# One core, a two-layer trunk in split float32: instructions recorded and issued in an order computed in the kernel, in place of the program's own order

## The chip, the cores and the metric

The kernel runs on one core of one Trainium2 chip. The metric is the device time of one execution in microseconds, the median of several runs.

Engine names as in the profile: PE is TensorE's matmul, PEld its weight load, DVE VectorE, ACT ScalarE, POOL GpSimd, SP SyncE, which here only issues DMAs. Each engine has an instruction queue of its own and works through it in order; an instruction that has to wait for another engine holds up what stands behind it on its own engine.

## The reference

Sequence 512, model width 1024, two layers, each a mixer followed by a SwiGLU FFN (hidden width 2816), each in front of a residual addition and behind an RMSNorm, and one RMSNorm at the end. The first mixer is a gated MLP whose gate mixes positions within chunks of 128, the second is retention with four heads. Everything is float32.

```python
for i in range(2):
    hn = rmsnorm(h, mix_norm_g[i])
    h = h + (sgu_mixer(hn, ...) if i == 0 else retention(hn, ...))
    h = h + swiglu(rmsnorm(h, ffn_norm_g[i]), ffn_w_gu[i], ffn_w_down[i])
return rmsnorm(h, final_norm_g)

# sgu_mixer: u, v = split(gelu(hn @ w_in)); v = layernorm(v); (u * (causal w_s @ v + b_s)) @ w_out
# retention: q, k, v, g = split(hn @ w_in); rotary(q), rotary(k); decayed causal attention by head;
#            (norm(o) * gn_g * silu(g)) @ w_out
# swiglu:    a, b = split(hn @ w_gu); (silu(a) * b) @ w_down
```

## The kernel before

**Split operands.** Each float32 operand is split in two: a high half, a copy rounded to the type that PE takes at its full pace (`fp32r`), made by ACT, and a low half, operand minus high half, made by DVE. Names with `wh_`/`wl_` are a weight's halves, `wr_` the raw weight, `XH`/`XL` those of the normed and transposed activations, `z_P6h`/`z_P6l` and the like those of sums of activations. `three` (lines 246 to 249) issues three matmuls for each pair of blocks: high by high (L247), and the two mixed products (L248, L249).

**Seven products.** A large product is done in quarters with seven block products instead of eight (`seven`): P1, P7, P6, Q4, P5, P2, P3. Each adds into one of three PSUM accumulators, X, Y and Z (in the last layer also W), and needs sums of weight blocks (P7 two blocks, P6 three, Q4 four, P5 two) and sums of activation quarters (S1 to S4; `z_S1`, `z_S2` in retention's output product). A weight sum is made either by DVE from two loaded tiles (`plus`, L377), or by an accumulating DMA which POOL issues onto the tile that holds the block before (`add`, L349), after the product that read that tile has made its halves. Plain loads go through SP (`load`, L346). All weight tiles come from one pool of 38 tiles of 4 KB a partition.

**Stages.** The SGU mixer: products `v0`, `v1`, `u0`, `u1` and the mixing, then `so`, which adds into the residual X. FFN 0: six units `gu0_0` to `gu0_5`, then `dn0_0` and `dn0_1`, which add into X. Retention: per head queries and keys (`qk`), values and gate (`vg`), scores, `pv`, then `zT`, the transpose of the gated result, then `ro`, which adds into X. FFN 1: `gu1_*`, `dn1_0`, `dn1_1`; its end norm runs by chunks inside the last product (`apart`), and the result is stored.

**The turn.** In front of each layer the residual of a chunk of 128 rows is scaled (`xs_f0_3` for chunk 3 in front of FFN 0), transposed by PE in eight pieces into PSUM (`xT_f0_3`), and copied out (`turn`, L667 to L672): ACT makes XH's columns, DVE XL's, both from PSUM, and for FFNs and retention `raw_copy` (L704) makes two float32 copies `xr`, from which the sums of activation quarters are built. These copies free the PSUM bank.

**What sets the order.** The program issues work as jobs with leads: `pipeline` calls a weight's load 8 jobs ahead of its product, its high half 6, its low half 5, its sum 7, an accumulating DMA 8 and more. Products follow one of four written orders (`ORDER`, `LATER`, `FIRST`, `SPREAD`). The order of the instructions that results is then scheduled again by the framework (`schedule_with_timeline_sim=True`), which moves instructions within the limits of their dependences, and gives each engine its queue.

Of the kernel before, what the change touches and what calls it, by code (L numbers as in the profile page):

```python
# [32 lines left out]
N_GEN = 38  # L33
N_TMP = 5
# [22 lines left out]
class Job:  # L57
# [34 lines left out]
def pipeline(jobs):  # L92
    weighted = [j for j in jobs if j.steps]
    leads = sorted({n for j in weighted for n, _ in j.steps})
    at = dict.fromkeys(leads, 0)
    done = 0
    for job in jobs:
        for n in leads if done else leads[::-1]:
            while at[n] < min(len(weighted), done + n):
                for m, step in weighted[at[n]].steps:  # L100
                    if m == n:
                        step()
                at[n] += 1
        if job.steps:
            done += 1
        if job.work:
            Chain.all_step()
        job.run()


@with_exitstack
def trunk(ctx, tc, x, positions, mix_g, ffn_g, fin_g, sgu_w_in, sgu_w_s, sgu_b_s, sgu_ln_g, sgu_ln_b,
          sgu_w_out, ret_w_in, ret_gn_g, ret_w_out, ffn_w_gu, ffn_w_down, invf, decay, out):
    nc = tc.nc
    const = ctx.enter_context(tc.tile_pool(name="const", bufs=1))
# [35 lines left out]
    def f32(t):  # L151
        return t.bitcast(F32)
# [6 lines left out]
    late = []  # L159
# [3 lines left out]
            late.pop(0)()  # L163

    ident = const.tile([P, P], F32, name="ident")
    make_identity(nc, ident)
# [84 lines left out]
    xn = {}  # L251
# [265 lines left out]
    def into_x(name, w, groups, A, ready=None, mid=None, look=3, halves=(0, 1), apart=False):  # L517

        norm = chunk_norm(name, ready, with_gain if apart else None) if ready else None
        by_dma = norm and sum(len(up) for up, low in groups) == 4

        def plus(i, j, ps, op, cs=(0, 1)):
            c0 = 2 * halves[i]
            q = X[:, c0 + cs[0]:c0 + cs[-1] + 1, j * T:(j + 1) * T]
            nc.vector.tensor_tensor(q, q, ps[:, cs[0]:cs[-1] + 1, :], op)

        def dma_plus(q, i, j, ps, sign):
            t = G(f"{q}_{name}")  # L530
# [132 lines left out]
    def turn(c, src, name, more=None):  # L663

        ps = PS(f"xT_{name}_{c}", (P, KD, P))
        for k in range(KD):
            xn["turned"] = nc.tensor.transpose(ps[:, k, :], src[:, k * P:(k + 1) * P], ident)  # L667
# [3 lines left out]
        nc.scalar.activation(xn["h"][:, :, cs], ps, AF.Copy)  # L671
# [23 lines left out]
    XR = {}  # L695

    def raw_copy(name):

        def copy(c, ps):
            if (name, c // 2) not in XR:  # L700
                XR[name, c // 2] = [G(f"xr_{name}_{c // 2}_{j}", F32, (P, 4, H)) for j in range(2)]
            cs = slice((c % 2) * P, (c % 2 + 1) * P)
            for j in range(2):
                nc.scalar.activation(XR[name, c // 2][j][:, :, cs], ps[:, 4 * j:4 * j + 4, :], AF.Copy)  # L704
# [124 lines left out]
    v = [[None, None] for _ in range(2)]  # L829
# [149 lines left out]
    def mix(j, half):  # L979
        for i in (2 * half, 2 * half + 1):  # L980
# [10 lines left out]
            if i % 2 == 1:  # L991
# [288 lines left out]
    t = [list(range(4 * hd, 4 * hd + 4)) for hd in range(HEADS)]  # L1280
# [39 lines left out]
```

## Time and profile before

| what | value |
|---|---|
| median of 3 runs | 1202.3 us (1201.9 to 1203.36) |
| the profiled execution's own time | 1203.41 us |
| its span | 1201.7 us, 18455 instructions |
| mean granted clock of PE | 0.996 |
| PE busy | 1180.0 us, 98% |
| DVE, ACT, POOL busy | 960.9 (80%), 664.6 (55%), 171.0 us (14%) |
| bytes moved by DMA | 225.90 MB, 188 GB/s over the span |

The span is the time from the first instruction to the last of one profiled execution; the profiled execution's own time has what lies around that span as well. A busy share is an average over stages that wait for different things. Where PE idles, the profile names the engine, line and tile that ended the wait (the "waits"), and the granted clock (1.00 is full speed) shows whether a busy PE is also a fast one.

### The profile page before, as it was taken

To read this page: it belongs to the slowest core of one execution; us is meant where nothing else is said; L and a number is where in the kernel's file an instruction comes from. 1 tells how busy PE (TensorE), PEld (TensorE's weight loads), DVE (VectorE), ACT (ScalarE), POOL (GpSimd) and SP (SyncE) were. 2 spreads that over 40 slices of the span, in tenths; PEclk is the share of its full clock that TensorE was granted. 3 is DMA by queue.
4 is the path that set the end of the run, shared out by engine and by line. 5 is a ranking of instruction groups with operands and counts; after the bars stand their busy time and mean duration, and the time that the engine had idled before them with its cause. 6 is when DMAs were issued, how large, how long until landed. Compare 5 with 4: busy or idle time off the path is not lost.

```text
span 1201.7 us, 18455 instructions
## 1 busy us (share of the span) xinstructions
PE 1180.0 (98%) x7374; PEld 1067.4 (89%) x7374; DVE 960.9 (80%) x1143; ACT 664.6 (55%) x842; POOL 171.0 (14%) x151
## 2 busy tenths in 40 slices
PE   8999999999999999999999999999999999999997
PEld 7888899989999987988989898878899989999986
DVE  5587998899977789787885959879788896676897
ACT  5523775554444547555664656566565545535465
POOL 1000122121010130110201111220121210101210
PEclk9999999999999999999999999999999999999999
DMA  9912878898684898777677868877868887856892
GB/s 314 282 47 59 244 161 182 226 228 208 160 205 108 225 184 265 176 163 184 155 202 178 192 155 203 183 151 247 217 153 211 186 216 210 199 135 192 168 245 97
DMA packets 128167, 225.90 MB, mean 188 GB/s; under 512 B 7464, under 2 KB 30032, under 8 KB 128080
## 3 DMA queue, kind: packets, MB, share of 16 engines
q1 hardware_dynamic: 88848, 153.37, 38.6%
q0 software_dynamic: 38944, 70.81, 35.3%
q8 instruction: 58, 0.95, 0.3%
q10 hardware_dynamic: 288, 0.52, 0.1%
q14 instruction: 29, 0.24, 0.1%
HBM read 221.53 MB, written 2.10 MB: 186 GB/s over the span
## 4 chain that ended last, share of the span: by engine, by line
PE 85%; DMA 5%; issue 4%; DVE 2%; ACT 2%; POOL 1%; SPq 0%; DVEq 0%; POOLq 0%; ACTq 0%
PE X_gu L247 6%; PE X_gu L249 6%; PE X_gu L248 6%; DMA wr_gu_P<-in_ffn_w_gu 3%; PE Y_gu L249 3%; PE Y_gu L248 3%; PE Y_gu L247 3%; PE X_dn L247 3%; PE X_dn L248 3%; PE X_dn L249 3%; PE X_vg L247 2%; PE X_vg L248 2%; PE X_vg L249 2%; PE ps_v L247 1%; PE Y_dn L248 1%
## 5 line engine op out<-in xcount | busy, mean ns | idle before, releaser
L216 ACT ACTIVATE wh_gu_P<-wr_gu_P 128x1024 fp32r<-128x1024 f32 x132 | 135.3, 1053 | 87.6 <-DVE wr_gu_P L377 51.0
L223 DVE TENSOR_TENSOR wl_gu_P<-wr_gu_P,wh_gu_P 128x1024 fp32r<-128x1024 f32 x132 | 158.7, 1219 | 25.4 <-ACT wh_gu_P L216 25.1
L349 POOL DMA_DIRECT2D wr_gu_P<-in_ffn_w_gu x50 | 60.9, 1258 | 414.0 <-DVE wl_gu_P L223 196.2
L216 ACT ACTIVATE wh_dn_P<-wr_dn_P 128x1024 fp32r<-128x1024 f32 x72 | 69.1, 980 | 42.6 <-DMA wr_dn_P<-in_ffn_w_down 17.8
L223 DVE TENSOR_TENSOR wl_dn_P<-wr_dn_P,wh_dn_P 128x1024 fp32r<-128x1024 f32 x72 | 79.4, 1128 | 2.7 <-issue 1.1
L223 DVE TENSOR_TENSOR wl_vg_P<-wr_vg_P,wh_vg_P 128x1024 fp32r<-128x1024 f32 x48 | 57.8, 1217 | 14.5 <-ACT wh_vg_P L216 14.4
L349 POOL DMA_DIRECT2D wr_dn_P<-in_ffn_w_down x36 | 41.9, 1239 | 143.6 <-DVE wl_dn_P L223 46.6
L216 ACT ACTIVATE wh_vg_P<-wr_vg_P 128x1024 fp32r<-128x1024 f32 x48 | 49.2, 1055 | 22.8 <-DMA wr_vg_P<-in_ret_w_in 16.7
L349 POOL DMA_DIRECT2D wr_vg_P<-in_ret_w_in x26 | 31.5, 1248 | 207.5 <-DMA wr_vg_P<-in_ret_w_in 73.8
L247 PE MATMUL X_gu<-XH_f,wh_gu_P 128*128 128x256 f32 x176 | 50.6, 288 | 2.2 <-ACT xr_f L704 2.2
L247 PE MATMUL Z_gu<-XH_f,wh_gu_P 128*128 128x256 f32 x176 | 50.0, 284 | 1.4 <-DVE s L1051 1.4
L247 PE MATMUL X_gu<-xP5h_f,wh_gu_P 128*128 128x256 f32 x176 | 50.0, 284 | 0.9 <-ACT u L1026 0.9
L249 PE MATMUL Y_gu<-XH_f,wl_gu_Q 128*128 128x256 f32 x176 | 49.9, 284 | 0.8 <-DVE wl_gu_Q L223 0.8
L248 PE MATMUL X_gu<-XL_f,wh_gu_P 128*128 128x256 f32 x176 | 50.5, 287 | 0.0
L249 PE MATMUL X_gu<-XH_f,wl_gu_P 128*128 128x256 f32 x176 | 50.5, 287 | 0.0
L247 PE MATMUL X_gu<-xP6h_f,wh_gu_P 128*128 128x256 f32 x176 | 50.0, 284 | 0.2
L247 PE MATMUL Y_gu<-XH_f,wh_gu_Q 128*128 128x256 f32 x176 | 49.9, 284 | 0.0
L249 PE MATMUL Z_gu<-XH_f,wl_gu_P 128*128 128x256 f32 x176 | 49.9, 283 | 0.0
L248 PE MATMUL X_gu<-xP6l_f,wh_gu_P 128*128 128x256 f32 x176 | 49.8, 283 | 0.0
L249 PE MATMUL X_gu<-xP3h_f,wl_gu_P 128*128 128x256 f32 x176 | 49.8, 283 | 0.0
L248 PE MATMUL X_gu<-xP3l_f,wh_gu_P 128*128 128x256 f32 x176 | 49.8, 283 | 0.0
L249 PE MATMUL X_gu<-xP6h_f,wl_gu_P 128*128 128x256 f32 x176 | 49.8, 283 | 0.0
(643 smaller groups left out, 4284.5 us busy)
## 6 DMA issues: line engine op xcount, KB each, us to landing
wr_gu_P<-in_ffn_w_gu SPq DMA_DIRECT2D x110, 512.0 KB, 5.3
wr_gu_P<-in_ffn_w_gu POOLq DMA_DIRECT2D x50, 512.0 KB, 7.8
wr_dn_P<-in_ffn_w_down SPq DMA_DIRECT2D x50, 512.0 KB, 5.5
wr_vg_P<-in_ret_w_in SPq DMA_DIRECT2D x40, 512.0 KB, 5.8
wr_dn_P<-in_ffn_w_down POOLq DMA_DIRECT2D x30, 512.0 KB, 7.3
wr_vg_P<-in_ret_w_in POOLq DMA_DIRECT2D x26, 512.0 KB, 6.9
wr_ro_P<-in_ret_w_out SPq DMA_DIRECT2D x20, 512.0 KB, 4.8
wr_qk_P<-in_ret_w_in SPq DMA_DIRECT2D x15, 512.0 KB, 5.9
```

Of the source, the lines that this page charges most:

```text
L216: nc.scalar.activation(h, s, AF.Copy)
L223: nc.vector.tensor_tensor(l, s, f32(h), ALU.subtract)
L247: nc.tensor.matmul(o, ah, bh, start=start, stop=False, skip_group_check=True)
L248: nc.tensor.matmul(o, ah, bl, start=False, stop=False, skip_group_check=True)
L249: return nc.tensor.matmul(o, al, bh, start=False, stop=stop, skip_group_check=True)
L349: nc.gpsimd.dma_start(raw[p, 0, g, s][:, 0:nk, :], source(b, g, s, nk), accum_op=ALU.add)
```

## The change

Three edits.

1. **Order.** Every call on an engine is recorded instead of issued (`Recorder`, `EngineProxy`, `record`); tiles are stand-ins (`Virtual`, `View`) which know who reads and writes which part. At the end, `emit` computes an order from fixed costs for each kind of instruction and issues all of it in this order, with the framework's own scheduling off. The order is made in two passes. Backward from PE's program order, every other operation gets the latest time at which it may end (`late`). Then a forward pass plays the engines against each other: PE takes the lowest program number among what is ready; the others the operation with the least `late`; at most 8 DMAs each on SP and on POOL are taken to be under way; a transfer counts as landed 2000 (the pass counts in ns) after its planned landing, so that its readers stand later in their queues. Tiles of a pool are granted in this order too. The waits themselves are still semaphores: the numbers only set the order of the queues. In the changed kernel the recorded operations all bear the line 332.

```diff
+HW_DMAS = 8
+LATE = 2000
...
+        else:
+            q = min(active, key=lambda q: q[0][1])
+            op = q.pop(0)[0]
+            op.end = now
+            post(now + LATE, op)
...
+                if e == "PE":
+                    op = min((o for o in queue[e] if can(o)), key=lambda o: o.n, default=None)
+                else:
+                    for o in queue[e]:
+                        if can(o):
...
+                            cost = o.late + (3 * TABLE if o.table and o.table != table else 0)
+                            if op is None or (cost, o.n) < best:
+                                op, best = o, (cost, o.n)
...
+def emit(rec):
+    with rec.tc.manual_schedule():
+        for op in order_of(rec):
+            op.call()
...
     pipeline(jobs)
+    emit(rec)
```

2. **XL from copies.** Where a turn also makes `xr` copies (the turns f0, r and f1, four chunks each), XL's columns are no longer made from PSUM by one DVE subtraction of 1024 columns but from the two `xr` copies in SBUF by two of 512.

```diff
         nc.scalar.activation(xn["h"][:, :, cs], ps, AF.Copy)
-        nc.vector.tensor_tensor(xn["l"][:, :, cs], ps, f32(xn["h"][:, :, cs]), ALU.subtract)
-        if more is not None:
-            more(c, ps)
+        if more is None:
+            nc.vector.tensor_tensor(xn["l"][:, :, cs], ps, f32(xn["h"][:, :, cs]), ALU.subtract)
+        else:
+            more(c, ps, cs)
...
-                nc.scalar.activation(XR[name, c // 2][j][:, :, cs], ps[:, 4 * j:4 * j + 4, :], AF.Copy)
+                nc.scalar.activation(own[j], ps[:, 4 * j:4 * j + 4, :], AF.Copy)
+            for j in range(2):
+                js = slice(4 * j, 4 * j + 4)
+                nc.vector.tensor_tensor(xn["l"][:, js, cs], own[j], f32(xn["h"][:, js, cs]), ALU.subtract)
```

3. **The last product's P5.** In `dn1_1` the sum of two blocks for P5 is made by an accumulating DMA onto a tile of its own instead of by a DVE addition: four DVE additions fewer, four POOL DMAs more.

```diff
-            made = seven(name, w, groups, 0, T, A, evac, mid, look, order=order, dma=("P7",), onto=("P6", "Q4"), apart=apart,
+            made = seven(name, w, groups, 0, T, A, evac, mid, look, order=order, dma=("P7", "P5") if apart else ("P7",), onto=("P6", "Q4"), apart=apart,
```

Of instructions, the matmuls and SP's loads are the same in number; ACT has 17 table loads instead of 14.

What the order became at three places. DVE at the second half of retention's output product (`ro`): `sg3_*` are the last head's gated results, `X_95` (`X_82` in the changed kernel) is the residual, `z_S1_1`, `z_S2_1` and `z_P6l_1` are what P6's second half needs. Before:

```order
L1236 SCALAR_TENSOR_TENSOR sg3_0_7406<-pv3_0_7607,nf5_o3_0_7626,sg3_0_7406 128x512 x2
L527 TENSOR_TENSOR X_95<-X_95,Y_ro_7684 128x2x512
L223 TENSOR_TENSOR wl_ro_P6_1_0_7700<-wr_ro_P722_1_0_7431,wh_ro_P6_1_0_7699 128x1024
L480 TENSOR_TENSOR z_S1_1_7749<-z2_1_7009,z3_1_7714 128x1024
L480 TENSOR_TENSOR z_S2_1_7751<-z_S1_1_7749,z2_0_7023 128x1024
L223 TENSOR_TENSOR wl_ro_P6_1_2_7745<-wr_ro_P722_1_2_7457,wh_ro_P6_1_2_7744 128x1024
L506 TENSOR_TENSOR z_P6l_1_7748<-z_S2_1_7751,z_P6h_1_7747 128x1024
```

After:

```order
L332 SCALAR_TENSOR_TENSOR sg3_1_7497<-pv3_1_7558,nf5_o3_1_7688,sg3_1_7497 128x512 x2
L332 SCALAR_TENSOR_TENSOR sg3_0_7556<-pv3_0_7581,nf5_o3_0_7690,sg3_0_7556 128x512 x2
L332 TENSOR_TENSOR wl_ro_P6_1_0_7718<-wr_ro_P722_1_0_7433,wh_ro_P6_1_0_7703 128x1024
L332 TENSOR_TENSOR z_S2_0_7637<-z_S2_0_7637,z1_0_6397 128x1024
L332 TENSOR_TENSOR X_82<-X_82,s1_ro_7684 128x2x512
L332 TENSOR_TENSOR z_S1_1_7758<-z2_1_7037,z3_1_7734 128x1024
L332 TENSOR_TENSOR wl_ro_Q4_0_0_7769<-wr_ro_P722_0_0_7330,wh_ro_Q4_0_0_7752 128x1024
L332 TENSOR_TENSOR z_S2_1_7776<-z_S1_1_7758,z2_0_7057 128x1024
L332 TENSOR_TENSOR wl_ro_P6_1_2_7785<-wr_ro_P722_1_2_7512,wh_ro_P6_1_2_7760 128x1024
L332 TENSOR_TENSOR X_82<-X_82,Y_ro_7669 128x2x512
L332 TENSOR_TENSOR z_P6l_1_7803<-z_S2_1_7776,z_P6h_1_7790 128x1024
```

The addition of Y_ro to the residual stood ahead of z_S1 and z_S2 and now stands behind them, directly in front of z_P6l. On PE, Y_ro's second P7 half and the first P6 half of X_ro (24 matmuls each) stand between the transposes of the last head and the product that reads z_P6l_1.

ACT at the turn into FFN 1 (`f1`): the copies out of the transposes of the last two chunks, `xT_f1_0` and `xT_f1_1`. Before:

```order
L671 ACTIVATE XH_f1_8143<-xT_f1_0_8370 128x8x128
L216 ACTIVATE wh_gu1_1_P1_0_2_8302<-wr_gu1_1_P111_0_2_8229 128x1024
L216 ACTIVATE wh_gu1_1_P2_0_0_8333<-wr_gu1_1_P221_0_0_8237 128x1024
L1026 ACTIVATE s1_1_0_8361<-X_gu1_0_8307 128x1024
L216 ACTIVATE wh_gu1_1_P2_0_2_8364<-wr_gu1_1_P221_0_2_8305 128x1024
L704 ACTIVATE xr_f1_0_0_8381<-xT_f1_0_8370 128x4x128
L671 ACTIVATE XH_f1_8143<-xT_f1_1_8446 128x8x128
L704 ACTIVATE xr_f1_0_1_8382<-xT_f1_0_8370 128x4x128
L216 ACTIVATE wh_gu1_0_P7_0_0_8411<-wr_gu1_0_P722_0_0_8231 128x1024
L1052 ACT_TABLE_LOAD
L1052 ACTIVATE s1_1_0_8361<-s1_1_0_8361 128x1024
L216 ACTIVATE wh_gu1_0_P7_0_2_8443<-wr_gu1_0_P722_0_2_8239 128x1024
```

After:

```order
L332 ACTIVATE s1_1_0_8395<-X_gu1_0_8284 128x1024
L332 ACTIVATE XH_f1_8189<-xT_f1_0_8392 128x8x128
L332 ACTIVATE xr_f1_0_0_8416<-xT_f1_0_8392 128x4x128
L332 ACTIVATE xr_f1_0_1_8422<-xT_f1_0_8392 128x4x128
L332 ACTIVATE wh_gu1_0_P6_0_0_8430<-wr_gu1_0_P722_0_0_8088 128x1024
L332 ACTIVATE wh_gu1_0_P5_0_0_8468<-wr_gu1_0_P512_0_0_8263 128x1024
L332 ACTIVATE xr_f1_0_0_8416<-xT_f1_1_8465 128x4x128
L332 ACTIVATE XH_f1_8189<-xT_f1_1_8465 128x8x128
L332 ACTIVATE xr_f1_0_1_8422<-xT_f1_1_8465 128x4x128
L332 ACTIVATE xP7h_f1_8503<-xP7_f1_8488 128x1024
L332 ACTIVATE wh_gu1_0_P6_0_2_8515<-wr_gu1_0_P722_0_2_8146 128x1024
L332 ACTIVATE xP5h_f1_8529<-xP5_f1_8509 128x1024
```

XH and the two xr copies of a chunk, which stood mixed with weight halves, now stand next to each other. On PE, the 48 matmuls of FFN 1's first Z_gu follow directly behind these transposes.

DVE at the turn into FFN 0 (`f0`): `nf3` to `nf5` are steps of the norm's factor for chunks 3 and 2, `xs_f0_3` and `xs_f0_2` the scaled chunks which PE transposes next. Before:

```order
L659 TENSOR_SCALAR nf4_so_3_1206<-nf3_so_3_1205 128x1
L655 SCALAR_TENSOR_TENSOR nf3_so_2_1225<-nf2_so_2_1224,nf0_so_2_1222 128x1
L660 TENSOR_TENSOR nf5_so_3_1207<-nf4_so_3_1206,nf2_so_3_1204 128x1
L659 TENSOR_SCALAR nf4_so_2_1226<-nf3_so_2_1225 128x1
L685 SCALAR_TENSOR_TENSOR xs_f0_3_1216<-X_95,nf5_so_3_1207,g_f0_1214 128x1024
L660 TENSOR_TENSOR nf5_so_2_1227<-nf4_so_2_1226,nf2_so_2_1224 128x1
L527 TENSOR_TENSOR X_95<-X_95,Z_so_1242 128x2x512
L685 SCALAR_TENSOR_TENSOR xs_f0_2_1234<-X_95,nf5_so_2_1227,g_f0_1214 128x1024
```

After:

```order
L332 TENSOR_SCALAR nf4_so_3_1283<-nf3_so_3_1278 128x1
L332 TENSOR_TENSOR X_82<-X_82,Z_so_1218 128x2x512
L332 TENSOR_TENSOR nf5_so_3_1291<-nf4_so_3_1283,nf2_so_3_1273 128x1
L332 TENSOR_SCALAR nf4_so_2_1294<-nf3_so_2_1280 128x1
L332 TENSOR_TENSOR wl_gu0_1_P1_0_2_1298<-wr_gu0_1_P111_0_2_1174,wh_gu0_1_P1_0_2_1271 128x1024
L332 SCALAR_TENSOR_TENSOR xs_f0_3_1306<-X_82,nf5_so_3_1291,g_f0_1025 128x1024
L332 TENSOR_TENSOR nf5_so_2_1310<-nf4_so_2_1294,nf2_so_2_1275 128x1
L332 TENSOR_TENSOR X_82<-X_82,X_so_976 128x512
L332 SCALAR_TENSOR_TENSOR xs_f0_2_1319<-X_82,nf5_so_2_1310,g_f0_1025 128x1024
```

The addition of Z_so to the residual, which waits for PE, stood between the two scalings; it and a weight's low half now stand in front of both. On PE, 12 matmuls of P3 stand between the end of Z_so and the first transpose; behind the second transpose stand 7 more matmuls ahead of the first that reads XH and XL.

Two more places in words. On PE, in FFN 0, the second half's Z_gu product stood 18 matmuls deep ahead of the 48 of X_gu's first product; now all of its 48 stand behind those. On SP, at the start, the first chunk of X (two loads of 256 KB) stood ahead of the two 256 KB loads of the first weight tile, and the second chunk directly behind them; now the loads of that weight tile and of the first chunk alternate, and the 512 KB load of the second weight tile stands ahead of the second chunk.

More of the change, by code (lines that the diff above doesn't have):

```diff
@@ L108, in pipeline, with __init__, view, __getitem__ @@
         job.run()
+ENGINE_OF = {"tensor": "PE", "vector": "DVE", "scalar": "ACT", "gpsimd": "POOL", "sync": "SP"}
+RESULT = 35
+TO_PE = 55
+HW_DMAS = 8
+class Virtual:
+    def __init__(self, rec, pool, shape, dtype, tag, name, bufs, psum):
+        import numpy as np
+        self.rec, self.pool, self.dims, self.dtype, self.tag, self.name, self.bufs = rec, pool, list(shape), dtype, tag, name, bufs
+        free = 1
+        for n in self.dims[1:]:
+            free *= n
+        self.grain = free if psum else max(1, free // 64)
+        self.index = np.broadcast_to(np.arange(free).reshape([1] + self.dims[1:]), self.dims)
+        self.users, self.left, self.real, self.history, self.granted, self.when = [], 0, None, [], None, None
+        self.first = None
+    def view(self):
+        return View(self, self.index, ())
+    def __getitem__(self, key):
+        return self.view()[key]
+    def __getattr__(self, name):
+        if name.startswith("_"):
+            raise AttributeError(name)
+        return getattr(View(self, self.index, ()), name)
+    def realize(self):
+        if self.real is None:
+            extra = {} if self.tag is None else {"tag": f"{self.tag}_{self.granted}", "bufs": 1}
+            self.real = self.pool.real.tile(self.dims, self.dtype, name=self.name, **extra)
+        return self.real
@@ new lines, with __init__, tile, pool @@
+class Pool:
+    def __init__(self, rec, real, bufs, psum):
+        self.rec, self.real, self.bufs, self.psum = rec, real, bufs, psum
+    def tile(self, shape, dtype, tag=None, name=None, bufs=None):
+        return Virtual(self.rec, self, shape, dtype, tag, name, bufs, self.psum)
+class Op:
+    __slots__ = ("n", "engine", "call", "before", "after", "tiles", "new", "busy", "took", "table", "kind", "start", "end",
+                 "late", "left", "ready", "ins", "what", "slow", "then")
+class Recorder:
+    def __init__(self, tc):
+        self.tc, self.real = tc, tc.nc
+        self.ops, self.held = [], {}
+        for attr in ENGINE_OF:
+            setattr(self, attr, EngineProxy(self, attr))
+    def pool(self, real, bufs, psum=False):
+        return Pool(self, real, bufs, psum)
+    def add(self, engine, call, reads, writes, what, busy, took, table=None, kind=None, slow=0):
+        op = Op()
+        op.n, op.engine, op.call, op.what, op.busy, op.took, op.table, op.kind = len(self.ops), engine, call, what, busy, took, table, kind
+        op.before, op.after, op.then, op.tiles, op.new, op.ins, op.slow = set(), [], [], [], [], None, slow
+        seen = set()
+        for views, w in ((reads, False), (writes, True)):
+            for v in views:
+                t, m = v.tile, v.mask()
+                for q, qm, qw in t.history:
+                    if q is not op and (w or qw or t.pool.psum and q.engine != engine) and qm & m:
+                        op.before.add(q)
+                if id(t) not in seen:
+                    seen.add(id(t))
+                    op.tiles.append(t)
+                    t.users.append(op)
+                    if t.first is None:
+                        t.first = op
+                        op.new.append(t)
+                        if t.pool.psum:
+                            was = self.held.get(t.tag)
+                            self.held[t.tag] = t
+                            op.before.update(was.users if was else ())
+        for views, w in ((reads, False), (writes, True)):
+            for v in views:
+                t, m = v.tile, v.mask()
+                if w:
+                    t.history = [h for h in t.history if h[1] & ~m]
+                t.history.append((op, m, w))
+        for q in op.before:
+            (q.then if q.engine == engine == "PE" else q.after).append(op)
+        self.ops.append(op)
+        return op
+    def issue_after(self, ins):
+        return nullcontext()
+    def high_priority(self):
+        return nullcontext()
@@ new lines, in record, with call @@
+def record(self, attr, name, args, kwargs):
+    args = [as_view(a) for a in args]
+    kwargs = {k: as_view(a) for k, a in kwargs.items()}
+    writes, reads = [], []
+    if "out" in kwargs:
+        writes.append(kwargs["out"])
+    elif args:
+        writes.append(args[0])
+    if "accum_out" in kwargs:
+        writes.append(kwargs["accum_out"])
+    if "accum_op" in kwargs:
+        reads.append(args[0])
+    reads += [a for a in args[1:] if isinstance(a, View)]
+    reads += [a for k, a in kwargs.items() if isinstance(a, View) and k not in ("out", "accum_out")]
+    writes = [w for w in writes if isinstance(w, View)]
+    engine = ENGINE_OF[attr]
+    table = kind = None
+    slow = 0
+    n = writes[0].width() if writes else reads[0].width()
+    psum = any(r.tile.pool.psum for r in reads)
+    if name == "dma_start":
+        kind = "add" if "accum_op" in kwargs else "load" if writes else "store"
+        size = n * 4 * (writes or reads)[0].shape[0]
+        busy = {"SP": 450, "POOL": 1200, "ACT": 100}[engine]
+        took = busy
+        slow = max(60, size * (2 if kind == "add" else 1) * 1400 // 524288)
+    elif name == "transpose":
+        busy, took = 109, 275
+    elif engine == "PE":
+        n = args[2].width()
+        busy = 4 * n // 2.4 if args[2].tile.dtype == F32 else max(60, n / 2.4 + 13.5)
+        busy = int(busy)
+        took = busy + 166
+    elif engine == "DVE":
+        inputs = [r for r in reads if r.width() > 1 or n == 1]
+        two = name in ("tensor_tensor", "scalar_tensor_tensor", "bn_stats") or psum
+        busy = int(66 + (1.042 if two else 0.524) * (reads[0].width() if name == "bn_stats" else n))
+        if name == "scalar_tensor_tensor" and isinstance(args[2], View):
+            busy += 60
+        took = busy + 84
+    elif engine == "ACT":
+        func = args[2]
+        busy = int(90 + 0.835 * n) + (95 if "accum_out" in kwargs else 0)
+        took = busy + 120 + (95 if "accum_out" in kwargs else 0)
+        table = None if func in (AF.Copy, AF.Square) else str(func)
+        if isinstance(kwargs.get("scale"), View):
+            busy, took = int(88 + 1.03 * n), int(178 + 1.03 * n)
+    else:
+        busy = took = int(100 + 1.4 * n)
+    fn = getattr(getattr(self.real, attr), name)
+    def call():
+        return fn(*[real_of(a) for a in args], **{k: real_of(a) for k, a in kwargs.items()})
+    what = f"{name} {(writes or reads)[0].tile.name}"
+    return self.add(engine, call, reads, writes, what, busy, took, table, kind, slow)
@@ new lines, with backward, post, settle @@
+Recorder.record = record
+LAND = 2200
+MARGIN = 600
+TABLE = 1400
+FLIGHT_HW = 2100
+FLIGHT_SW = 3100
+LATE = 2000
+POOL_DATA = 640
+POOL_RESULT = 400
+def backward(ops, lazy, total, gap):
+    import heapq
+    events, serial = [], 0
+    free, pending = {}, {}
+    need, left = {}, {}
+    def post(back, op):
+        nonlocal serial
+        serial += 1
+        heapq.heappush(events, (back, serial, op))
+    def settle(op):
+        for q in op.before:
+            if q.engine != "PE":
+                need[q] = min(need.get(q, total), op.late - gap(op, q))
+                left[q] -= 1
+                if left[q] == 0:
+                    ready(q)
+    def ready(q):
+        place = "dma" if q.kind else q.engine
+        by = need.get(q, total) - (MARGIN if q.kind else q.took - q.busy)
+        pending.setdefault(place, []).append((q, total - by))
+        post(total - by, None)
+    for op in ops:
+        if op.engine != "PE":
+            left[op] = len(op.after)
+    for op in reversed(ops):
+        if op.engine == "PE":
+            post(total - op.late, op)
+        elif not op.after:
+            ready(op)
+    while events:
+        back, _, op = heapq.heappop(events)
+        if op is not None:
+            settle(op)
+        if events and events[0][0] == back:
+            continue
+        for place, queue in pending.items():
+            if free.get(place, back) > back:
+                continue
+            able = [q for q, at in queue if at <= back]
+            if not able:
+                continue
+            q = max(able, key=lambda o: (lazy[o], o.n))
+            queue[:] = [e for e in queue if e[0] is not q]
+            length = q.slow if q.kind else q.busy
+            free[place] = back + length
+            post(free[place], None)
+            q.late = total - back - length - (LAND + q.busy if q.kind else 0)
+            post(total - q.late, q)
@@ L165, in trunk @@
     ident = const.tile([P, P], F32, name="ident")
-    make_identity(nc, ident)
+    rec.add("POOL", lambda: make_identity(rec.real, ident.realize()), [], [ident.view()], "identity", 600, 600)
     ones = const.tile([P, P], F32, name="ones")
@@ L671, in turn @@
         nc.scalar.activation(xn["h"][:, :, cs], ps, AF.Copy)
-        nc.vector.tensor_tensor(xn["l"][:, :, cs], ps, f32(xn["h"][:, :, cs]), ALU.subtract)
-        if more is not None:
-            more(c, ps)
+        if more is None:
+            nc.vector.tensor_tensor(xn["l"][:, :, cs], ps, f32(xn["h"][:, :, cs]), ALU.subtract)
+        else:
+            more(c, ps, cs)
         return ps
```

199 lines of the change are left out of this document (189 added, 10 removed).

## The prediction

> **What bounds the kernel now.** I read the page's first lines, then the chain's shares, then what PE waited for, then the granted clock behind the longest waits, and last the timelines of the engines that ended them.
>
> ```profile
> span 1201.7 us, 18455 instructions
> PE 1180.0 (98%) x7374; PEld 1067.4 (89%) x7374; DVE 960.9 (80%) x1143; ACT 664.6 (55%) x842; POOL 171.0 (14%) x151
> PE 85%; DMA 5%; issue 4%; DVE 2%; ACT 2%; POOL 1%; SPq 0%; DVEq 0%; POOLq 0%; ACTq 0%
> ```
>
> PE is busy 98% and carries 85% of the chain. The change leaves every matmul as it is, so nearly all of the span cannot move; the question is how much of PE's idle time, and of its slow time, goes away, and what new waits come. DVE at 80% is the engine with the least slack behind PE. All of PE's waits that the profile lists:
>
> ```profile
> PE xT_in L667 <- DMA X<-in_x: 2.2, 1, 2.2
> PE X_gu L247 <- ACT xr_f L704: 2.2, 1, 2.2
> PE X_ro L247 <- ACT z_P6h L502: 1.6, 1, 1.6
> PE Z_gu L247 <- DVE s L1051: 1.4, 1, 1.4
> PE wake L176 <- POOL eps L170: 1.2, 1, 1.2
> PE X_vg L247 <- ACT sg L1214: 1.0, 1, 1.0
> PE X_gu L247 <- ACT u L1026: 0.9, 2, 0.6
> PE Y_gu L249 <- DVE wl_gu_Q L223: 0.8, 1, 0.8
> PE X_ro L249 <- DVE z_P6l L506: 0.5, 1, 0.5
> PE Y_vg L249 <- DVE xP7l_r L743: 0.5, 1, 0.5
> PE Y_dn L247 <- ACT wh_dn_Q L216: 0.5, 1, 0.5
> PE X_vg L247 <- ACT xr_r L704: 0.5, 1, 0.5
> PE X_dn L247 <- ACT wh_dn_P L216: 0.5, 1, 0.5
> ```
>
> Leave out the two of the start (xT_in, wake): the eleven rows that remain sum to 10.4 us in 12 waits, each at a hand-over from ACT or DVE, none at a landed transfer. Two of them have a second price, which the clock shows (columns: stretch, length, PE busy with its matmul count, granted clock, DMA share, GB/s):
>
> ```profile
> 876.60:880.60 4.00, 4.00 (x23) 0.57 0.01 4
> 881.00:885.00 4.00, 4.00 (x35) 1.00 0.74 164
> 808.90:812.30 3.40, 3.40 (x10) 0.50 1.10 271
> 813.00:816.40 3.40, 3.40 (x17) 1.00 0.78 213
> ```
>
> Behind the 2.2 us wait of X_gu, 23 matmuls ran in 4 us where 35 run right after: 4.00 x 12/35 = 1.4 us lost. Behind the two waits of X_ro, 10 ran where 17 do: 3.40 x 7/17 = 1.4 us. So 10.4 + 2.8 us, and a little at each restart, is the stock that a better order can draw on.
>
> **The waits that the change takes away.** First retention's output product, with the chain through it (start, length, what):
>
> ```profile
> 801.04 0.24 PE Y_ro L249
> 801.30 1.22 DVE X L527
> 802.52 1.14 DVE wl_ro_P L223
> 803.66 1.15 DVE z_S L480
> 805.97 1.22 DVE wl_ro_P L223
> 807.19 1.22 DVE z_P6l L506
> 808.45 0.50 PE X_ro L249
> ```
>
> The DVE queue runs in order. The addition of Y_ro to X stands ahead of z_S1, z_S2 and z_P6l, and it can't start until PE has ended Y_ro; X_ro's P6 then waits for z_P6h and z_P6l. In the changed order z_S1 and z_S2 stand ahead of that addition, and PE has 24 + 24 matmuls (Y_ro's second half, X_ro's first P6 half) between zT3_0 and the first that wants z_P6l of the second half: 48 x 0.227 = 10.9 us, the pitch being that of the rows after 812.6. What DVE and ACT have to do meanwhile is eight pieces of at most 1.22 us, 9.8. It fits, closely. The 1.6 and 0.5 us go, and the 1.4 of clock. The last row also shows the restart: 0.50 where 0.24 is usual, so 0.25 a wait.
>
> Second, the last transposes before FFN 1:
>
> ```profile
> 874.64 1.03 ACT L671 ACTIVATE XH_f<-xT_f 128x1024 fp32r<-128x1024 f32 x1
> 875.54 0.62 ACT L704 ACTIVATE xr_f<-xT_f 128x512 f32<-128x512 f32 x1
> 876.21 0.38 PE L247 MATMUL X_gu<-XH_f,wh_gu_P 128*128 128x256 f32 x1 [2.18 <-ACT xr_f L704]
> ```
>
> PE waits for the copies out of the transposes' PSUM banks, since X_gu takes one of them; ACT had put weight halves and an s copy between them. In the changed order the three copies of a bank stand next to each other, 1.03 + 0.62 + 0.62 = 2.3 us, and DVE no longer reads the bank. Z_gu's 48 matmuls, 5.8 us at 0.12, stand ahead of X_gu. The 2.2 us and the 1.4 of clock go. Third, Z_gu's 1.4 us for s in FFN 0: the changed order puts the 48 matmuls of the next X_gu half (5.8 us) ahead of the Z_gu product that waited, where 18 stood. Gone.
>
> Gone with good ground: 2.2 + 1.6 + 0.5 + 1.4 = 5.7; four restarts 1.0; clock 2.8: **9.5 us**. The other seven rows (4.7 us in eight waits, 2.0 of restarts: 6.7) are late weight or activation halves. Counted over the whole program, the PE work between a DVE result and its first use is 12.3 us in the median where it was 6.8, and leads under 2.4 us fall from 84 to 51 (on ACT 51 to 22), by matmul counts times the pitches above. I take 5.0 of the 6.7 as gone, between 2 and 6.7.
>
> **The waits that it adds.** At the turn into FFN 0 the f0 rows stand thus:
>
> ```profile
> 142.41 1.28 DVE L685 SCALAR_TENSOR_TENSOR xs_f<-X,nf_so,g_f 128x1024 f32<-128x1024 f32 x1
> 144.42 1.22 DVE L527 TENSOR_TENSOR X<-X,Z_so 128x1024 f32<-128x1024 f32 x1 [0.65 <-PE Z_so L249]
> 146.75 1.22 DVE L223 TENSOR_TENSOR wl_gu_P<-wr_gu_P,wh_gu_P 128x1024 fp32r<-128x1024 f32 x1
> 146.95 1.91 PE L667 MATMUL xT_f<-ident,xs_f 128*128 128x128 f32 x16
> ```
>
> Before, xs_f of chunk 3 (142.41) is made ahead of X += Z_so (144.42). In the changed order that addition, which waits for PE, and one weight low half stand ahead of xs_f. From the end of Z_so: 1.14 + 0.13 + 1.14 + 1.28 = 3.7 us (starts of neighbouring rows lie 0.08 closer than the lengths), while PE has 12 matmuls of P3, 12 x 0.227 = 2.7. So xT_f waits about 1.0 us, and as only 7 matmuls stand behind the second xT_f, its XH and XL come about another 1.0 late. I take 2.0, between 0 and 3.
>
> ```profile
> 2.67 5.39 DMA X<-in_x
> 0.00:25.00 25.00, 21.47 (x93) 17.82 (x94) 15.22 (x33) 13.71 (x20) 5.60 (x14) 1.00 0.94 324
> ```
>
> At the start the DMA engines are full (0.94, 324 GB/s) and PE waits 2.2 us for the second chunk of X, landing at 8.06. On SP's queue 512 KB of the second weight tile now go ahead of that chunk: 0.524 MB at 324 GB/s is 1.6 us. Little else can be put before it. I take 1.5, between 0 and 3 (3: the first matmuls' slow-clock stretch also grows).
>
> For hand-overs that the new order makes just in time elsewhere I set 1.0, between 0 (none) and 8 (as many as the old 6.7 and the clock of one). It is near the low end because the leads grew.
>
> **The edits that cost nothing.** The XL parts made from copies are two DVE subtractions of 512 columns instead of one of 1024, 12 times: the row X<-X,X_so of 512 columns lies at 0.68 beside 1.22, so 12 x 0.14 = 1.7 us more on DVE, hidden by PE except at the two turns counted above. The last product's P5 by four accumulating loads takes four additions of 1.2 us off DVE:
>
> ```profile
> 1150.00:1180.00 30.00, 30.00 (x134) 24.86 (x133) 29.51 (x32) 19.49 (x28) 2.14 (x2) 1.00 0.74 213
> 1180.00:1202.00 22.00, 14.03 (x62) 11.27 (x61) 13.71 (x39) 10.15 (x21) 0.00 (x0) 0.91 0.26 96
> ```
>
> There DVE is at 29.51 of 30 us, but PE isn't idle for a moment, so the 4.8 us are no gain; the loads go onto a DMA share of 0.74. Three more ACT table loads of about 1.3 us lie on an engine at 55%. The order behind the last matmul is the same in both programs: 0 for the tail.
>
> **Sum.** -9.5 - 5.0 + 2.0 + 1.5 + 1.0 = -10.0. The profiled execution has a span of 1201.7 and took 1203.41, 1.1 above the median of 1202.3 (1201.9 to 1203.36). The new span would be 1191.7, the median **1192**.
>
> [...] The rows show half clock behind a single wait of 2.2 us and behind 1.6 + 0.5, and none behind the 1.4. [...]
>
> **Rivals.** (A, slower) *Accumulating loads land late.* In these rows an accumulating load takes longer than a plain one:
>
> ```profile
> wr_gu_P<-in_ffn_w_gu SPq DMA_DIRECT2D x110, 512.0 KB, 5.3
> wr_gu_P<-in_ffn_w_gu POOLq DMA_DIRECT2D x50, 512.0 KB, 7.8
> ```
>
> The new order issues plain loads earlier and keeps more of them in flight on the same DMA engines; if that stretches the accumulations (they are serial: each sum reads what the one before left, and the last serves Q4), the halves of Q4, P6 and P5 come late. 50 such adds serve the FFNs' first products alone; if 25 of their readers come 0.5 us late for PE the gain of 10 is gone, and at 0.7 with the half clock of four of them (1.4 each) the result is 1202.3 - 10 + 17.5 + 5.6 = 1215. Against it: none of PE's waits before is for a landing, and matmul work between an add and its reader grows from 10.4 to 12.7 us in the median, under 6 us in 13 cases instead of 30. It decides from about 12.4 us in all.
>
> (B, same) *The new order has as many just-in-time places as the old one*, only elsewhere: the third sum at its upper end of 8 and 2 of the 6.7 gone: -9.5 - 2 + 2 + 1.5 + 8 = 0: 1202.
>
> (C) *Nearly all waits go and none come*: -9.5 - 6.7 = -16.2: 1186. For it: the leads. Against it: the order at f0 and at the start.
>
> [...]
>
> **Chances.** The forecast, with terms at their ends, 1188 to 1199: 0.57. C 0.16, D 0.07, B 0.07, A 0.13. A change of 0.2% (2.4 us) is about what a measurement of this kernel can tell from none, so faster (below 1199.9) 0.80, same 0.07, slower (above 1204.7) 0.13. The range takes in C and B and leaves out most of A: 1185 to 1203.
>
> **What the changed profile would show.** Right: no wait at X_ro, at the first X_gu of FFN 1 or at Z_gu behind s, and a clock of 1.00 in the stretches that were at 0.50 and 0.57; a new wait of PE at xT_f of FFN 0 ended by DVE's xs_f, of about 1 us; the first wait for X longer by about 1.5 us; the last 30 us with DVE well under 29.5 and PE as before; the sum of PE's waits (without the start) near 4 instead of 10.4. Wrong: PE waits ended by DMA landings or by wh and wl of Q4 and P5 tiles, POOL landings well over 7.8 us, or a half clock without a wait ahead of it.

## The result and the profile after

The changed kernel takes 1195.07 us (median of 4 runs, 1194.42 to 1195.63) against 1202.83 (4 runs, 1201.9 to 1203.48) for the kernel before: a ratio of 0.9936, 95% interval 0.9919 to 0.9953, so 7.8 us or 0.6% faster. The forecast was 1192 in a range of 1185 to 1203. The first lines of the page after, and the shares of its chain:

```profile
span 1193.8 us, 18464 instructions
PE 1176.7 (99%) x7374; PEld 1063.5 (89%) x7374; DVE 959.7 (80%) x1151; ACT 678.6 (57%) x845; POOL 175.2 (15%) x155
PE 85%; DVE 8%; DMA 3%; ACT 2%; issue 1%; SPq 0%; DVEq 0%; ACTq 0%
```

The matmuls are the same in number and the span is 7.9 us shorter. What PE waits for now (engine, tile, releaser: total, times, longest):

```profile
PE wake L332 <- POOL ones L332: 2.3, 1, 2.3
PE xT_in L332 <- DMA X<-in_x: 1.5, 2, 0.7
PE xT_f L332 <- DVE xs_f L332: 1.3, 1, 1.3
PE X_dn L332 <- ACT s_dn L332: 1.2, 1, 1.2
PE ps_v L332 <- ACT XH_in L332: 1.1, 1, 1.1
PE X_gu L332 <- ACT u L332: 0.8, 2, 0.5
PE Z_gu L332 <- ACT xr_f L332: 0.5, 1, 0.5
PE xT_r L332 <- DVE nf_dn L332: 0.4, 1, 0.4
PE X_gu L332 <- DVE XL_f L332: 0.3, 1, 0.3
PE sc L332 <- DVE k0l L332: 0.2, 1, 0.2
```

The waits behind the start are 4.7 us where they were 10.4. X_gu behind u is the only one of the old list that is left; the others are new. By stages, PE's busy time and clock, first before, then after (turn into and first part of FFN 0; end of FFN 0 and start of retention; retention's output product; turn into FFN 1; and the start, of after alone):

```profile
140.00:200.00 60.00, 57.14 (x431) 1.00 0.84 199
430.00:545.00 115.00, 113.06 (x603) 1.00 0.81 200
760.00:830.00 70.00, 66.92 (x297) 0.98 0.79 183
860.00:910.00 50.00, 47.35 (x366) 0.97 0.79 176
```

```profile
140.00:200.00 60.00, 57.36 (x428) 1.00 0.82 192
430.00:545.00 115.00, 113.25 (x605) 1.00 0.75 184
760.00:830.00 70.00, 70.00 (x319) 1.00 0.83 198
860.00:910.00 50.00, 49.74 (x415) 1.00 0.85 194
0.00:25.00 25.00, 20.09 (x82) 1.00 0.93 328
```

The gain comes from two places. At retention's output product PE's idle 3.1 us became none, at the turn into FFN 1 2.65 became 0.26, and the half clock of both (0.50 at X_ro, 0.57 at X_gu, together 2.8 us) is gone. The other two stages are about as idle as before (2.9 to 2.6, 1.9 to 1.75), with other waits; the first 25 us have 1.4 us less of busy PE (21.47 before). So far the forecast's picture held, and the theory at this point was: the order makes the gain, the two small edits nothing. The rival was that the edits carry a share.

### The profile page after: what moved, and what is told of

Its sections match the earlier page's. It is cut to its first block, busy times and chain, and to the rows that moved or that the text cites. A ratio compares the mean times of both kernels' runs of the same rounds, so it can differ in the third digit from the quotient of the medians.

```text
span 1193.8 us, 18464 instructions
## 1 busy us (share of the span) xinstructions
PE 1176.7 (99%) x7374; PEld 1063.5 (89%) x7374; DVE 959.7 (80%) x1151; ACT 678.6 (57%) x845; POOL 175.2 (15%) x155
## 4 chain that ended last, share of the span: by engine, by line
PE 85%; DVE 8%; DMA 3%; ACT 2%; issue 1%; SPq 0%; DVEq 0%; ACTq 0%
PE X_gu L332 20%; PE Y_gu L332 9%; PE X_dn L332 7%; PE X_vg L332 6%; PE Z_gu L332 5%; PE Y_dn L332 4%; PE ps_v L332 4%; PE ps_u L332 4%; PE X_ro L332 4%; PE Y_vg L332 3%; PE X_qk L332 3%; DMA wr_gu_P<-in_ffn_w_gu 2%; PE pv L332 2%; PE Y_ro L332 2%; PE Z_dn L332 2%
## 5 line engine op out<-in xcount | busy, mean ns | idle before, releaser
L332 ACT ACTIVATE wh_gu_P<-wr_gu_P 128x1024 fp32r<-128x1024 f32 x132 | 137.8, 1057 | 119.4 <-DMA wr_gu_P<-in_ffn_w_gu 33.5
L332 ACT ACTIVATE wh_dn_P<-wr_dn_P 128x1024 fp32r<-128x1024 f32 (+1 forms) x72 | 69.7, 983 | 44.3 <-PE X_gu L332 12.9
L332 DVE TENSOR_TENSOR wl_dn_P<-wr_dn_P,wh_dn_P 128x1024 fp32r<-128x1024 f32 (+1 forms) x72 | 80.6, 1131 | 17.6 <-ACT wh_dn_P L332 12.4
L332 POOL DMA_DIRECT2D wr_dn_P<-in_ffn_w_down x40 | 46.3, 1181 | 167.4 <-DMA wr_dn_P<-in_ffn_w_down 81.1
L332 PE MATMUL X_gu<-xP3h_f,wh_gu_P 128*128 128x256 f32 x176 | 50.3, 286 | 0.0
L332 PE MATMUL Z_gu<-XL_f,wh_gu_P 128*128 128x256 f32 x176 | 49.9, 283 | 0.0
L332 PE MATMUL Y_gu<-xP7h_f,wh_gu_P 128*128 128x256 f32 x176 | 49.8, 283 | 0.0
L332 PE MATMUL Y_gu<-xP7h_f,wl_gu_P 128*128 128x256 f32 x176 | 49.8, 283 | 0.0
L332 PE MATMUL Y_gu<-XL_f,wh_gu_Q 128*128 128x256 f32 x176 | 49.8, 283 | 0.0
```

The source lines that it names most:

```text
L332: return fn(*[real_of(a) for a in args], **{k: real_of(a) for k, a in kwargs.items()})
```

## The experiments

The kernel before was run again beside each set; ratios are to it. The changed kernel's own is 0.9936.

**e1: the order alone.** Both small edits undone.

```diff
-        if more is None: ... else: more(c, ps, cs)
+        nc.vector.tensor_tensor(xn["l"][:, :, cs], ps, f32(xn["h"][:, :, cs]), ALU.subtract)
...
-dma=("P7", "P5") if apart else ("P7",)
+dma=("P7",)
```

> The changed kernel with its order computed as there, but XL made from PSUM by one subtraction of 1024 columns and the last product's P5 summed by four DVE additions, as before the change. If the order alone carries the gain: 1194 to 1196, as the changed kernel (1195.1), since both other edits only move DVE work that PE covers. If the two other edits carry a share, because a bank is freed earlier at the turns: 1197 to 1199, with waits of PE for DVE's XL at the turns into FFN 0 and FFN 1.

Measured: 1202.54, ratio 1.0005 (0.9996 to 1.0014). Neither expectation: all of the gain is gone. Its waits of PE in the last product, and the clock there:

```profile
PE Z_dn L332 <- DVE h_P2l L332: 2.4, 1, 2.4
PE Z_dn L332 <- ACT h_P2h L332: 1.8, 1, 1.8
PE Z_dn L332 <- DVE wl_dn_P L332: 0.8, 1, 0.8
1141.00:1148.00 7.00, 4.65 (x11) 0.52 1.12 236
```

5.0 us of waits, and nearly 7 us at half clock with the longest of these waits inside it, at a place where neither the kernel before nor the changed one waits at all. The theory fell here.

**e2: the two edits alone**, on the old order.

```diff
+        if more is None: ... else: more(c, ps, cs)
...
+dma=("P7", "P5") if apart else ("P7",)
```

> The kernel before, in its own order, with only the two small edits (XL from the copies, P5 of the last product by accumulating loads). If the order alone carries the gain: 1201 to 1204, within 0.2% of the kernel before, with the waits for z_P6h and xr_f still there. If the edits carry a share: 1198 to 1200, and the wait of X_gu for xr_f in FFN 1 shorter than 2.2.

Measured: 1200.01, ratio 0.9980 (0.9972 to 0.9989): 2.2 us faster, a share but a small one (the framework schedules anew, so other pieces moved too). The old waits are there:

```profile
PE X_ro L247 <- ACT z_P6h L502: 1.6, 1, 1.6
PE X_gu L247 <- ACT xr_f L705: 1.5, 1, 1.5
```

Behind the waits of X_ro, where the kernel before ran at half clock (0.50), this trace shows full clock:

```profile
803.90:807.30 3.40, 3.40 (x17) 1.00 1.11 269
```

So the 2.2 us may be the clock's and need not be the edits' own. With e1 this says that order and edits work together: 0 and 2 us apart, 7.8 together.

**e5: only P5's sums back on DVE. e6: only XL back from PSUM.** Each takes one of the two edits of e1's diff.

> The changed kernel with only the P5 sums of the last product back on DVE. The order alone had brought nothing (1202.5 with both small edits undone), with 5 us of waits and 3 us of half clock at Z_dn of the last product. If that product's P5 is what the order needs: 1199 to 1203, with the waits at Z_dn again. If XL from PSUM was the cause: 1194 to 1197 and no wait at Z_dn.

> The changed kernel with only XL made from PSUM again. In the run with both small edits undone the turn into FFN 0 lost 5.0 us against 2.9 in the changed kernel. If XL costs only there: 1196 to 1198, with a wait for xr_f or XL_f and a stretch of half clock between 150 and 165 us. If P5 and XL only work together: 1199 to 1203.

Measured: e5 1202.1, ratio 1.0008 (0.9999 to 1.0017); e6 1193.61, ratio 0.9932 (0.9920 to 0.9945). e6 is below both of its ranges: XL from copies is worth nothing that can be measured. P5 by loads is worth the whole gain in the new order. e5's waits are e1's:

```profile
PE Z_dn L332 <- DVE h_P2l L332: 2.4, 1, 2.4
PE Z_dn L332 <- ACT h_P2h L332: 2.1, 1, 2.1
PE Z_dn L332 <- DVE wl_dn_P L332: 0.5, 1, 0.5
```

Z_dn is P2. Only 0.5 of the 5.0 us is for a weight half; 4.5 are for the halves of P2's activations, `h_P2h` and `h_P2l`, which ACT and DVE had put behind other work. DVE's additions for P5 are not what PE waits for: in e5 the first of the four comes 11 us behind the last of these waits.

```profile
1158.16 1.22 DVE L332 TENSOR_TENSOR wr_dn_P<-wr_dn_P,wr_dn_P 128x1024 f32<-128x1024 f32 x1
```

The order on PE is another, too. The changed kernel does P6 (X_dn, from 1138.6 us) ahead of P2 (Z_dn, from 1148.1); e5 starts P2 (1137.9) ahead of P6 (1147.2). P6 adds to the accumulator that holds P1's result, so it needs the copy `s_dn` of that result first, and this copy takes a tile of the pool of 38. The copy in the changed kernel and in e5:

```profile
1137.17 1.03 ACT L332 ACTIVATE s_dn<-X_dn 128x1024 f32<-128x1024 f32 x1 [0.91 <-PE Y_dn L332]
```

```profile
1145.95 1.02 ACT L332 ACTIVATE s_dn<-X_dn 128x1024 f32<-128x1024 f32 x1 [3.59 <-PE Z_dn L332]
```

In e5 the copy waits for a matmul of Z_dn, whose result it doesn't read; what is left for it to wait for is a tile. SP's loads are late as well. SP's loads from 1120 us on (start, length of the group) and the wait ahead of them, and PE's first matmul of Y_dn, the product P7, first in the changed kernel, then in e5:

```profile
SPq L332 <- PE X_dn L332: 23.6, 3, 18.8
1122.43 16.72 SPq L332 DMA_DIRECT2D wr_dn_P<-in_ffn_w_down  x6
1129.03 0.39 PE L332 MATMUL Y_dn<-wh_dn_P,h_P7h 128*128 128x512 f32 x1
```

```profile
SPq L332 <- DVE h_S L332: 23.7, 1, 23.7
1126.84 9.33 SPq L332 DMA_DIRECT2D wr_dn_P<-in_ffn_w_down  x4
1126.12 0.39 PE L332 MATMUL Y_dn<-wh_dn_P,h_P7h 128*128 128x512 f32 x1
```

In the changed kernel P2's first load goes out 6.6 us ahead of P7's first matmul, in e5 0.7 behind it. Ahead of P2's first load SP has waited 18.8 us for a matmul of P1 in the changed kernel, and 23.7 us for a DVE operation on another tile (h_S) in e5: a load of this kind waits for a tile of the pool of 38. Where DVE makes P5's sum, it reads P1's four raw tiles again, so these stay taken from P1 to P5. That these four tiles cause all of this is an argument so far.

**e7 and e9: P5 by loads, but P1's tiles held.** The edit of e9 (e7 reads P1's tile alone):

```diff
 def low():
     lows[0]()
+    if apart and p == "P5":
+        t = small.tile([P, 1], F32, tag="held", name=f"held_{g}_{s}")
+        nc.vector.tensor_tensor(t, raw["P1", "11", g, s][:, 0, 0:1], raw["P5", 0, g, s][:, 0, 0:1], ALU.add)
```

> The changed kernel, P5 of the last product by loads, but DVE reads one column of each of P1's four raw tiles when P5's low halves are made (four DVE instructions of one column more), so these tiles stay taken from P1 to P5, as they do where DVE makes the sum. If the four tiles of the pool are what the sums by loads set free: 1199 to 1203, P2's loads later and PE waiting at Z_dn. If it is DVE's 4.8 us of additions: 1194 to 1196.

e7: 1193.38, ratio 0.9933 (0.9921 to 0.9946). It tells nothing on the tiles: the reads depend on P1's load alone, and the computed order put them there (the first at 1097.35 us), so no tile was held.

> The changed kernel, P5 of the last product by loads, and DVE reads one column of each of P1's four raw tiles together with one of P5's landed sum. The earlier try read P1's tiles alone, and the computed order put these reads right behind P1, so nothing was held; now they can't stand before P5's landing. If the four tiles of the pool are what the sums by loads set free: 1199 to 1203, P2's first load several us later and PE waiting at Z_dn. If it is DVE's 4.8 us of additions and what they do to the order: 1193 to 1196. Between: both.

e9: 1198.24, ratio 0.9982 (0.9971 to 0.9993). Just under the lower end of what the tiles were to bring back, and well above the other theory's.

```profile
PE X_dn L332 <- ACT s_dn L332: 3.9, 2, 2.7
1124.85 12.58 SPq L332 DMA_DIRECT2D wr_dn_P<-in_ffn_w_down  x5
1128.74 0.39 PE L332 MATMUL Y_dn<-wh_dn_P,h_P7h 128*128 128x512 f32 x1
```

P2's first load goes out 3.9 us ahead of P7, between the two others; s_dn, too, starts between the two others, at 1140.1. PE does not wait at Z_dn, where the expectation had it: P6 stands ahead of P2 as in the changed kernel, and PE waits 2.7 us in front of it for s_dn; behind that wait matmuls of 512 columns start 0.43 us apart, ahead of it 0.23. This profiled execution took 1201.18, 2.9 above the median, so it shows more loss than most. Holding four tiles, with DVE relieved of the additions, brings back 0.0046 of the 0.0072 in ratio between the changed kernel and e5, some 64%; the intervals leave room from a third to nearly all. The two are not quite alike: the reads come at 1175 us and hold the tiles longer than e5's sums, made from 1158 on. So held tiles do cost time here, and a late s_dn is common to both; that they are all of e5's loss is not shown, and the rest, through an order that came out otherwise, isn't separated.

**e11: LATE = 0**, readers planned at the landing and not behind it.

```diff
-LATE = 2000
+LATE = 0
```

> The changed kernel with readers planned right at the planned landing of a transfer (0 instead of 2000). If planning readers behind landings is what keeps PE from waiting: 1197 to 1205, with waits of PE for wh and wl halves in many places. If the landings are early enough anyway: 1193 to 1196.

Measured: 1218.79 (1210.89 to 1220.41), ratio 1.0130 (1.0104 to 1.0157): 23 us more than the changed kernel by the ratios and well above the range. Four of PE's waits, and then ACT's for landed weights in the changed kernel and in e11:

```profile
PE X_gu L332 <- ACT u L332: 5.4, 4, 2.4
PE pv L332 <- ACT osq L332: 2.4, 1, 2.4
PE X_gu L332 <- ACT s L332: 2.4, 2, 1.6
PE Y_dn L332 <- ACT wh_dn_Q L332: 2.0, 1, 2.0
```

```profile
ACT wh_gu_P L332 <- DMA wr_gu_P<-in_ffn_w_gu: 33.5, 23, 4.1
```

```profile
ACT wh_gu_P L332 <- DMA wr_gu_P<-in_ffn_w_gu: 54.4, 30, 4.4
ACT wh_vg_P L332 <- DMA wr_vg_P<-in_ret_w_in: 25.7, 10, 5.5
```

ACT waits 54.4 us for gu's weights instead of 33.5, and 25.7 for vg's instead of 6.8. PE's own waits behind the start name no landing, and only one of these four a weight half: the late ones are u, osq, s, results of ACT that PE needs soon. That they stood behind a weight copy waiting for its transfer is what the rows suggest; each case wasn't followed.

**e3 and e8: the turn into FFN 0.** Both put xs_f back ahead of other DVE work. e3 moves X += Z_so, one addition of X_so and the weight low half behind both xs_f (one chunk's norm is then taken before that addition, so its values differ); e8 restores the order of before.

```diff
+    after(xs2, z, x0, wl)                           # e3
+    ahead(z, n3, xs3); ahead(wl, m2, n2, xs2)       # e8
```

> The changed kernel with one piece of DVE's order altered at the turn into FFN 0: X += Z_so, one addition of X_so and the weight low half stand behind xs_f of chunks 3 and 2 instead of ahead. If these pieces cause the wait of xT_f (1.3 us and its restart): that wait goes, 1193 to 1194. Rival: the Z bank and the weight half come late in its place and the wait moves on by a few us: 1195, with a new PE wait for wl_gu or for X between 150 and 160 us.

> The changed kernel with DVE's order at the turn into FFN 0 as in the kernel before: xs_f of chunk 3 ahead of X += Z_so, xs_f of chunk 2 ahead of the weight low half; the additions keep their order among themselves. In the earlier try, which put X += X_so behind both, the wait of xT_f went and X_so waited 1.4 for that addition. If the pieces ahead of xs_f cause the wait: no wait of xT_f and none of X_so, 1193 to 1194. Rival: X_so waits for the addition in its place, by 0.5 to 1.5: 1194 to 1195.5.

Measured: e3 1193.76, ratio 0.9930 (0.9918 to 0.9941); e8 1196.01, ratio 0.9957 (0.9943 to 0.9972). In both the wait of xT_f is gone, and another stands there, of e3 and of e8:

```profile
PE X_so L332 <- DVE X L332: 1.4, 1, 1.4
```

```profile
PE X_so L332 <- DVE X L332: 2.7, 1, 2.7
```

By the waits the rival was right, in e8 above its size. By the time e3 lies in the first theory's range; the ratios of both overlap with the changed kernel's, so the times don't tell. The place costs PE 1.3 to 2.7 us in any of the three orders, since PE needs both xs_f and the additions within the same few microseconds.

**e4: SP's first loads as before.**

```diff
+    ahead(w[0], *x[:2])
+    ahead(w[2], *x[2:4])
```

> The changed kernel with SP's first loads in the order of the kernel before: the first chunk of X ahead of the first weight tile, the second chunk ahead of the second weight tile. If the load order costs what was forecast for the start (1.5 us): 1193 to 1194, PE 1.6 us further on at 25 us. Rival: the weight tile then lands later and PE waits for it instead: 1195 to 1196.

Measured: 1194.7, ratio 0.9940 (0.9928 to 0.9952), as the changed kernel. The wait moved (the profiled execution took 1197.51, the longest of the five):

```profile
PE ps_v L332 <- ACT XH_in L332: 3.8, 1, 3.8
```

XH_in stands behind two weight copies in ACT's queue, and the second of these waited 1.5 us for its landing: the late weight tile of the rival, which PE meets by way of ACT.

**e10: the copy s1 of dn0_1 earlier**, which PE's X_dn waited for.

```diff
+    for op in ops:
+        if op.what == "activation s1_dn0_1":
+            op.late -= 15000
```

> The changed kernel with the copy s1 of dn0_1 given an earlier latest time, so that it gets its tile of the pool sooner and stands 9 us earlier in ACT's queue; PE's X_dn waited 1.2 us for this copy. If the tile was what held the copy: the wait at X_dn goes, 1.4 less, 1192 to 1194. Rival: another tile comes late instead and PE waits for that: 1194 to 1196.

Measured: 1195.12, ratio 0.9949 (0.9934 to 0.9963). X_dn's wait is gone, and others stand in its place: ps_qk waits 0.9 for XL_r and X_vg 0.6 for wl_vg_P, where neither waited, and sc 0.6 instead of 0.2. The waits behind the start sum to 4.7 us as before; the rival was right.

**e12: a wait put in** at the turn into FFN 1.

```diff
+    a = at("ACT", "activation xr_f1_0_0")[0]
+    i = order.index(a)
+    order[i:i] = 14 * [a]
```

> The changed kernel with one ACT copy, the first xr of FFN 1's turn, done 14 times more (7 us of ACT), to make PE wait at a known place near 870 us, by some 2 us. If a wait of 2 us always brings a stretch at half clock: 1.4 to 1.7 us more than the wait, clock 0.50 for 3.4 us behind it. If it depends on where the wait falls: the wait alone, clock 1.00. In all 1196 to 1199.

Measured: 1201.21, ratio 0.9995 (0.9980 to 1.0010), above the range of both; the wait came out at 4.3 instead of 2. PE's wait, and its clock from the last 1.9 us of the wait on:

```profile
PE X_gu L332 <- ACT xr_f L332: 4.3, 1, 4.3
872.50:879.20 6.70, 4.79 (x22) 0.50 0.07 9
```

The half clock lasts 6.7 us here, twice as long as behind the 2.2 of the kernel before (3.4, from 877.1 to 880.5 us at 0.51). In e8, though, the 2.7 us wait fell into this stretch, and the clock stayed at 1.00, here and in the 3.4 us behind it:

```profile
148.00:151.40 3.40, 0.67 (x7) 1.00 0.27 48
```

So the wait's length alone doesn't decide.

## Why the prediction was right, and where it wasn't

**The waits that go (9.5 us).** Right, in place and size: no wait at X_ro, at FFN 1's first X_gu or at Z_gu behind s, and a clock of 1.00. The stages show 3.1 + 2.4 us of idle and 2.8 of clock gone; Z_gu's 1.4 went, too. The 2.8 is the least certain part: in e2 half clock is missing at X_ro with its waits in place.

**The other old waits (5.0 of 6.7).** Right: of 4.7 us idle 0.8 is left, so with six restarts some 5.4 went.

**f0 (2.0).** Right place, too small: xT_f 1.3, Z_gu behind xr_f 0.5 and X_gu behind XL_f 0.3 are 2.1, with three restarts of 0.25 2.9, the upper end of 3. The restarts were not counted. The picture behind the term, that pieces put ahead of xs_f cause it and could be moved, was too simple (e3, e8).

**Start (1.5).** The size was right (1.4 less of busy PE in 25 us), in part by luck: the wait for X, which was to grow, is shorter than before (1.5 against 2.2). PE's other two waits of the start make up for it, `wake` with 2.3 against 1.2 and ps_v with a new 1.1, so that all three grow by 1.5. How much of it is the load order is not shown; putting the loads back brought nothing (e4). The first matmuls are slow in both, at a granted clock of 1.00 in these rows: those of 512 columns start 0.43 us apart until about 14 us before and 15 us after, and 0.23 from there on. This slow stretch begins later by 1.1 us, with `wake`, and ends later by about as much.

**Just-in-time places elsewhere (1.0).** Too small: X_dn 1.2, xT_r 0.4 and sc 0.2 with their restarts are 2.6. With these sizes the sum is -9.5 - 5.4 + 2.9 + 1.4 + 2.6 = -8.0; the spans differ by 7.9.

**The edits that cost nothing.** XL: right (e6). P5 by loads, "the 4.8 us are no gain": wrong for the order that the change has. Without it the new order takes 1202.1, with it about 1195. (The additions are 4.3 us; one of the four is half as wide and takes 0.7.) DVE's row was the wrong one to read. The step asked which work is saved, and not how long its source tiles stay taken, which other loads and copies wait for. The sign set for this step, DVE well under 29.5 of 30 us near the end, did not come: the same stretch of work now lies 7.9 us earlier, and DVE is busy in all of it.

```profile
1142.10:1172.10 30.00, 30.00 (x134) 24.83 (x133) 30.00 (x33) 19.97 (x29) 4.14 (x4) 1.00 0.75 190
```

What P5 by loads is worth lies around the start of that stretch, at 1125 to 1150.

**The rivals.** A: POOL's landings for gu took 7.2 instead of 7.8 us, with no PE wait for them:

```profile
wr_gu_P<-in_ffn_w_gu SPq DMA_DIRECT2D x110, 512.0 KB, 4.8
wr_gu_P<-in_ffn_w_gu POOLq DMA_DIRECT2D x50, 512.0 KB, 7.2
```

Those for dn and vg took longer than before (8.0 against 7.3 us, 7.7 against 6.9), also with no PE wait for a landing.

B and C were further off than the forecast. D, the half clock staying where the waits go (2.8 us less gained), has the time that was measured, 1195, but by luck: the slow stretches did not stay, both places ran at full clock (1.00), and in e12 one of them came back behind a wait (0.50). But A's neighbour, loads and copies that come late because no tile is free, fits what e1, e5 and e9 met; the forecast hadn't this rival, though four tiles held in one product are enough for some two thirds of the gain to go (e9).

## What to carry to other kernels

An order computed from fixed costs is worth its allowance for what the costs don't know: 2000 ns behind each landing were worth 23 us here, three times the whole gain, and e11's rows suggest why: a copy that waited for its transfer (ACT 54.4 us for gu's weights, 33.5 in the changed kernel) held up what stood behind it on its engine. An edit that is hidden in time may still decide what is loaded and copied when: count for each operation also how long it keeps its source tiles out of the pool, and look at what the load queue waits for. And with little to spare behind PE (DVE busy 14.0 of 15 us from 140 us on, at e3's and e8's place, and 14.0 of 14 from 428 on, at e10's; a DMA share of 0.93 in the first 25, at e4's), moving one piece to cure one wait moved the wait (e3, e4, e8, e10); these four cures of waits of 1 to 1.5 us changed the ratio by -0.0006 to +0.0021.

## What the runs showed of the hardware

The clock was not expected to behave as it did: 2.2 us of idle PE (before, FFN 1) were followed by half speed for about 3.4 us (0.51), 4.3 us (e12) by 6.7, the last 1.9 of the wait among them (0.50), and 2.73 us within 3.4 (e8) by none (1.00). Nor is a wait's length or place enough to tell: behind the 2.7 us of e9 matmuls of 512 columns start 0.43 us apart from 1141.7 to 1146.0 us, against 0.23 ahead of the wait, and behind the two waits of X_ro the clock was 0.50 in the kernel before and 1.00 in e2. What starts a slow stretch, and what sets its length, these runs don't show.

PE's pace at a clock of 1.00, in the changed kernel: 24 matmuls of 512 `fp32r` columns in 5.44 us from 800.66 us on, 0.227 each, and eight float32 transposes of 128 columns in 0.80 us from 869.30 on, 0.10 each; a column of the second kind takes 1.8 times as long.
